# Attention stage of a hybrid decoder trunk: accumulators taken in the order of the text, one query tile less ahead of the key transposes

## The chip, the cores and the metric

The kernel runs on one core of a Trainium2 chip. The metric is the time of one execution on the device in microseconds (us), the median over runs. A core has a matrix engine (TensorE, PE), ScalarE (ACT), VectorE (DVE), GpSimd (POOL) and SyncE (SP). Each works through its own instructions in order, and semaphores order the engines among each other. Matmul results stand in accumulators (PSUM banks), from which ACT or DVE must take them before the bank serves again.

## The reference

One layer of a gated decoder trunk, for a prompt of 1024 tokens and 8 sample sequences of 8 tokens (1088 tokens in all), in float32. A normed, modulated input goes through one wide projection whose columns feed three branches: A (chunked gating), B (attention in a sliding window of 128) and C (mLSTM). Each branch output is gated, projected, and merged. The change lies in the stage that computes branch B, in which parts of A and the gate of B are computed as well:

```python
def sink_attention(qb, kb, vb, mask, sinks):
    logits = jnp.einsum('bnqkgd,bnskd->bnkgqs', qb, kb) * (B_HEAD_DIM ** -0.5)
    logits = jnp.where(mask[None, :, None, None], logits, -jnp.inf)
    mx = jnp.maximum(logits.max(axis=-1), snk)
    p = jnp.exp(logits - mx[..., None])
    den = p.sum(axis=-1) + jnp.exp(snk - mx)
    out = jnp.einsum('bnkgqs,bnskd->bnkgqd', p, vb) / den[..., None]

    q = rmsnorm(q.reshape(bsz, t, B_HEADS, B_HEAD_DIM), qn_g)
    k = rmsnorm(k.reshape(bsz, t, B_KV_HEADS, B_HEAD_DIM), kn_g)
    yb = swa_branch(...) * jax.nn.silu(b_g)
```

There are 8 query heads in 2 groups (one key/value head each), so 16 prompt steps (group, tile of 128 tokens) and 4 sample steps (group, half of the sequences).

## The kernel before, in words

The stages follow each other: start (modulation, norm), the mLSTM branch, its output gates, the attention stage (about 362 to 588 us of the profiled execution), then a long stage of projections and merging up to the output. float32 products are made from pairs of a high and a low half (`hh`/`hlo` for the input, `hl` for a weight slab, read from `raw` in four pieces of 256 KB, cast by ACT and subtracted by DVE).

In the attention stage the key and value tiles come first, with `k_norm` for three tiles at a time and `k_transpose(n)` for one: ACT copies the key tile to `kst`, PE transposes it into an accumulator (two transposes, one per group), ACT casts it to the high half of `KT`, DVE subtracts the low half. From the fourth key tile on, the order of PE is written out by hand (`manual_schedule`): what stands in the text in front is ahead on PE. The other engines' instructions are placed by a scheduler that plans with priorities (`tc.high_priority`) and a model of times.

By hand, a pipeline of steps runs: in round `i` the list `PLAN` calls phase `v` of step i-5, `s` of step i-2, `p` of step i-4, `q` of step i (`y` is only for the samples). Phase `q` transposes a query tile into an accumulator; ACT (high half `hi`) and DVE (low half `lo`) empty it in two rounds (L1074, L1075) into `QT`; in round 7 of a group the sample query tile follows into `QTs`. Phase `s` makes scores in two accumulators, which ACT (`Sm`, L1106) and DVE (copy_predicated, L1107) empty; then come the row maximum, four exps on ACT (L1115), the sum and four normalisations on ACT (L1123). Phase `p` transposes the probabilities and DVE writes them as `Pp` and `Pc`; phase `v` multiplies with the values, and ACT takes the result as `yo` and sends it out.

Between the phases stands `filler`, a sequence of other matmuls of fixed length from which each place takes so many columns (`FILL`): query tiles (`q_tile`, evicted by DVE into `qraw`), tiles of branch A (`av_tile`, into `vn`, with squares on ACT, L1265), and chunks of the gate of B (`bg_chunk`), which ACT evicts twice, as `tb` (tanh, L1236) and `zb` (L1238). POOL sends `zb` out, ACT's queue `yo`. `filler(0, ("q", g, n))` runs the sequence until query tile n of group g is done.

Accumulators: `pg` for filler (three banks), `pk` for key and query transposes and scores (three), `pu` for the transposed probabilities and the output (two). `gt` tiles (`tb`, `zb`, `yo`, `ts`) share five buffers in rotation.

```python
PLAN = ((6, "y", 0), (5, "v", 0), (2, "s", 0.3), (4, "p", 0.3), (0, "q", 0.4))
for n in range(3, 9):
    filler(0, ("q", 0, n - 2))
    k_transpose(n)
```

Of the kernel before, what the change touches and what calls it, by code (L numbers as in the profile page):

```python
# [15 lines left out]
NT = 1088  # L16
# [25 lines left out]
def trunk_kernel(ctx: ExitStack, tc: tile.TileContext, I, O):  # L42
# [37 lines left out]
    def ct(shape, name, dt=F32):  # L80
        return cp.tile(shape, dt, name=name)


# [105 lines left out]
    def gemm_tok_steps(whi, wlo, K, N, n, ah, al, evac):  # L189
        t0, tn = TILES[n]  # L190
        ps = pg()
        for k in range(K):
            if n == 8:
                mm(ps[:, :N], ah[k][:, 1024:1152], whi[:, k], k == 0, False)
                mm(ps[:, :N], ah[k][:, 1024:1152], wlo[:, k], False, k == K - 1)
            else:
                mm(ps[:tn, :N], ah[k][:, t0:t0 + tn], whi[:, k], k == 0, False)
                mm(ps[:tn, :N], ah[k][:, t0:t0 + tn], wlo[:, k], False, False)
                mm(ps[:tn, :N], al[k][:, t0:t0 + tn], whi[:, k], False, k == K - 1)
            if k < K - 1:  # L200
                yield N
        if n == 8:
            t = gt(N, "ts")
            with tc.high_priority():
                S.copy(t[:64], ps[64:128, :N])
                V.tensor_tensor(t[:64], t[:64], ps[:64, :N], ALU.add)
            ps = t
        evac(ps)
        yield N
# [671 lines left out]
    with tc.tile_pool(name="bph", bufs=1, side="right", reuse_waits="tile") as b1:  # L881
# [177 lines left out]
        def q_transpose(g, n):  # L1059
            tn = TILES[n][1]  # L1060
            pq = pk()
            for i in range(2):
                tr(pq[:, tn * i:tn * i + tn], qraw[g][i][:tn, n])
            QT = bt([128, 2, 2, 128], "QT", F32R, bufs=3) if n < 8 else bt([128, 8, 4, 8], "QTs", F32R, bufs=2)
            for r in range(2):
                a, b = slice(64 * r, 64 * r + 64), slice(64 - 64 * r, 128 - 64 * r)
                if n < 8:
                    src = pq[a, 0:256].rearrange("p (i t) -> p i t", i=2)
                    hi, lo = QT[a, :, r], QT[b, :, r]
                else:  # L1070
                    src = pq[a, 0:128].rearrange("p (i b t) -> p b i t", i=2, b=8)
                    hi, lo = QT[a, :, r::2], QT[b, :, r::2]
                with tc.high_priority():
                    S.copy(hi, src)  # L1074
                    newq[0] = V.tensor_tensor(lo, src, hi.bitcast(F32), ALU.subtract).ins  # L1075
            return QT.rearrange("p i r t -> p (i r t)")
# [4 lines left out]
        class Prompt:  # L1081
            def __init__(self, g, n):
                self.g, self.n = g, n
# [11 lines left out]
            def s(self):  # L1095
                g, n, QT, rr = self.g, self.n, self.QT, self.rr
                Sm = bt([128, 4, 128], "Sm", bufs=3)
                for hp_ in range(2):
                    pS = pk()
                    for i in range(2):  # L1100
                        h = 2 * hp_ + i
                        o = pS[:, 256 * i:256 * i + 256]
                        mm(o, QT[:, 128 * h:128 * h + 128], KT[g][0][:, 128 * n:128 * n + 256], True, False)
                        mm(o, QT[:, 128 * h:128 * h + 128], KT[g][1][:, 128 * n:128 * n + 256], False, True)
                    pv = pS.rearrange("p (i w s) -> p i w s", i=2, w=2)
                    S.copy(Sm[:, 2 * hp_:2 * hp_ + 2], pv[:, :, 1])  # L1106
                    V.copy_predicated(Sm[:, 2 * hp_:2 * hp_ + 2], mprv.unsqueeze(1).broadcast_to([128, 2, 128]),  # L1107
                                      pv[:, :, 0] if n > 0 else neg.unsqueeze(1).broadcast_to([128, 2, 128]))
# [17 lines left out]
            def p(self):  # L1126
                n = self.n
                pT = pu_()
                for h in range(4):
                    j = 2 * (h % 2) + h // 2  # L1130
                    tr(pT[:, 128 * j:128 * j + 128], self.Sm[:, h])
                pTv = pT.rearrange("p (h t) -> p h t", h=4)
                if n > 0:
                    self.Pp = bt([128, 4, 128], "Pp")
                    V.scalar_tensor_tensor(self.Pp, mcT.unsqueeze(1).broadcast_to([128, 4, 128]), 0.5, pTv,
                                           ALU.is_lt, ALU.mult)
                self.Pc = bt([128, 4, 128], "Pc")
                V.tensor_tensor(self.Pc, pTv, mcT.unsqueeze(1).broadcast_to([128, 4, 128]), ALU.mult)

            def v(self):  # L1140
# [6 lines left out]
                o = gt(256, "yo")  # L1147
                S.activation(o, pO[:, 0:256], AF.Copy, scale=0.5)
                nc.scalar.dma_start(dy[1, 2 * g:2 * g + 2, :, 128 * n:128 * n + 128].rearrange("f p t -> p f t"),
# [6 lines left out]
        class Sample:  # L1156
# [3 lines left out]
            def q(self):  # L1160
# [12 lines left out]
                self.kT = bt([128, 4, 128], "kTs", tag="QT", bufs=3)  # L1173
                V.tensor_copy(self.kT, pK.rearrange("p (b j) -> p b j", b=4))

            def s(self):
# [6 lines left out]
                Sx = bt([128, 192], "Sx", tag="Sm", bufs=3)  # L1183
                V.tensor_tensor(Sx[:, 0:128], pS[:, 0:128], smask[:, 0:128], ALU.add)
                V.tensor_tensor(Sx[:, 128:192], pS[:, 128:192], smask[:, 160:224] if bg == 0 else smask[:, 128:192], ALU.add)
                nm = bt([128, 1], "nms", bufs=2)
# [10 lines left out]
            def p(self):  # L1197
# [3 lines left out]
                self.PT = bt([128, 256], "PTs", tag="Pc")  # L1201
                V.tensor_copy(self.PT[:, 0:128], pT[:, 0:128])
                V.tensor_copy(self.PT[:64, 128:256], pT[0:64, 128:256])

            def v(self):
# [5 lines left out]
                self.ot = bt([128, 64], "ots", bufs=2)  # L1211
                V.tensor_copy(self.ot, pO[:, 0:64])
                V.tensor_tensor(self.ot, self.ot, pO[:, 64:128], ALU.add)
                V.tensor_scalar(self.ot, self.ot, self.dn, 0.5, ALU.mult, ALU.mult)

            def y(self):
# [3 lines left out]
                for r in range(2):  # L1220
                    S.copy(o[64 * r:64 * r + 64].rearrange("p f (b t) -> p b f t", t=8),
                           py[0:64, 0:128].rearrange("p (b f r t) -> p b f r t", f=2, r=2, t=8)[:, :, :, r])
# [5 lines left out]
        def bg_chunk(f, ci):  # L1228
# [5 lines left out]
            def ev_b(ci, c0, n, ps):  # L1234
                t = gt(n, "tb")
                S.activation(t, ps[:, :n], AF.Tanh, bias=bh[:, CBG + f:CBG + f + 1], scale=0.5)  # L1236
                z = gt(n, "zb")
                S.activation(z, ps[:, :n], AF.Identity, bias=cols[:, CBG + f:CBG + f + 1], scale=1.0)  # L1238
                V.scalar_tensor_tensor(z, t, 1.0, z, ALU.add, ALU.mult)
# [9 lines left out]
        def av_tile(s, n):  # L1249
# [9 lines left out]
            def ev_a(ps):  # L1259
                with tc.high_priority():  # L1260
                    for i in range(2):
                        g = 2 * s + i
                        V.tensor_tensor(vn[g][:tn, n], ps[:tn, 128 * i:128 * i + 128],
                                        avb["b", s][:tn, 128 * i:128 * i + 128], ALU.add)
# [54 lines left out]
        def mix(g):  # L1319
# [3 lines left out]
            for q in range(2):  # L1323
                ps = pk()
                for i in range(4):
                    mm(ps[:, 128 * i:128 * i + 128], vn[g][:, 4 * q + i], WT[:, g], True, True)
                V.scalar_tensor_tensor(sA[g][:, 512 * q:512 * q + 512].rearrange("p (n t) -> p n t", n=4),
                                       ps.rearrange("p (n t) -> p n t", n=4), gcol,
                                       bsb[:, g:g + 1].broadcast_to([128, 4, 128]), ALU.mult, ALU.add)
            ps = pk()  # L1330
            mm(ps[:, 0:64], vn[g][:64, 8], A["WTs"][:, g].rearrange("p b t -> p (b t)"), True, True)
            V.scalar_tensor_tensor(sA[g][:, 1024:NT].rearrange("p (b t) -> p b t", b=8),
                                   ps[:, 0:64].rearrange("p (b t) -> p b t", b=8), gcol,
# [14 lines left out]
        for n in range(9):  # L1348
# [36 lines left out]
        for n in range(3, 9):  # L1385
            filler(0, ("q", 0, n - 2))
            k_transpose(n)
# [19 lines left out]
    keep.close()  # L1407
    one.close()


# [499 lines left out]
```

## Time and profile before

| | |
|---|---|
| median of 3 runs | 1180.49 us (1179.37 to 1182.17) |
| profiled execution | 1182.86 us, its span 1181.1 us |
| mean granted clock of TensorE | 0.999 |
| PE, DVE, ACT busy | 1157.1, 789.1, 489.8 us |
| attention stage, 362 to 588 us: PE, DVE, ACT busy | 222.8, 164.4, 142.8 us |

The span runs from the first to the last instruction; the profiled execution's own time holds some time around it. PE's busy time is that of its matmuls. In a row of the timeline stand the start, the busy time, the engine, the line, the operation with output and inputs, the shapes and how many equal ones follow each other; brackets hold the idle time before it and what ended it. All matmuls have line L88 and all transposes L92, since two helpers record them.

### The profile page before, as it was taken

What the parts mean: (1) busy time and instruction counts of PE and PEld (TensorE: products, weight loads), DVE (VectorE), ACT (ScalarE), POOL (GpSimd) and SP (SyncE); (2) the same over time, 40 slices, a digit from 0 to 9 for tenths busy, and PEclk for the clock granted to TensorE, in tenths of its full rate; (3) what the DMA queues carried; (4) which work ended last, traced back from release to release, by engine and by line L of the source; (5) the groups of instructions that cost most, each with busy time, mean ns of one, the idle gap of its engine ahead of it and who ended that gap; (6) DMA issues with size and microseconds to landing.
All of it is one profiled execution on the core that took longest, in us unless ns stands there. A gap on an engine that the chain in (4) does not pass through costs nothing.

```text
span 1181.1 us, 23183 instructions
## 1 busy us (share of the span) xinstructions
PE 1157.1 (98%) x8942; PEld 1111.5 (94%) x8942; DVE 789.1 (67%) x1865; ACT 489.8 (41%) x1230; POOL 75.7 (6%) x109
## 2 busy tenths in 40 slices
PE   6999999999999999989999999999999999999998
PEld 4799999999999999978998999999999999999998
DVE  5778777655468587876698866555766676668433
ACT  4443455434343368877443433223332343235000
POOL 2000011102024010120100000000000000000000
PEclk9999999999999999999999999999999999999999
DMA  9731222323222211123235125545633354465322
GB/s 300 250 90 37 76 85 64 103 65 103 88 79 75 51 49 40 29 78 90 66 104 149 46 83 154 148 141 149 179 113 114 109 159 119 131 215 182 119 92 72
DMA packets 150773, 129.74 MB, mean 110 GB/s; under 512 B 13613, under 2 KB 140213, under 8 KB 150648
## 3 DMA queue, kind: packets, MB, share of 16 engines
q1 hardware_dynamic: 142984, 118.96, 34.2%
q0 software_dynamic: 2240, 7.08, 1.7%
q10 hardware_dynamic: 5440, 2.23, 0.7%
q8 instruction: 70, 1.15, 0.4%
q14 instruction: 39, 0.32, 0.1%
HBM read 99.39 MB, written 29.82 MB: 109 GB/s over the span
## 4 chain that ended last, share of the span: by engine, by line
PE 86%; DVE 7%; DMA 4%; ACT 2%; issue 1%; SPq 0%; POOL 0%; ACTq 0%; DVEq 0%
PE pg L88 46%; PE pk L88 24%; PE pu L88 13%; PE pk L92 2%; DMA raw<-in_w_in_dram 1%; DMA stage<-dy 1%; PE pu L92 1%; DVE acc L502 1%; DMA xt<-in_x_prompt_dram 1%; DVE hl L128 1%; DMA dy<-stage 0%; DMA fbb<-in_mlstm_f_bias_dram 0%; DVE vv L543 0%; DVE hl L413 0%; DMA mrow<-in_ada_b_dram 0%
## 5 line engine op out<-in xcount | busy, mean ns | idle before, releaser
L88 PE MATMUL pg<-hl,hl 128*128 128x256 f32 (+3 forms) x904 | 277.7, 307 | 0.6 <-DVE hl L413 0.3
L88 PE MATMUL pg<-hh,hl 128*128 128x384 f32 (+1 forms) x912 | 237.4, 335 | 0.4 <-DVE hh L412 0.4
L88 PE MATMUL pg<-hl,hh 128*128 128x256 f32 (+1 forms) x1008 | 177.7, 283 | 0.5 <-DVE zif L547 0.5
L88 PEld LDWEIGHTS pg<-hl,hl 128*128 128x128 f32 x904 | 170.6, 189 | 3.2 <-DVE hl L413 2.4
L88 PEld LDWEIGHTS pg<-hh,hl 128*128 128x128 f32 x912 | 161.8, 189 | 4.1 <-issue 1.9
L88 PEld LDWEIGHTS pg<-hl,hh 128*128 128x128 f32 x1008 | 150.7, 189 | 1.0 <-PE pg L88 0.7
L1441 ACT CAST prod<-raw 128x512 fp32r<-128x512 f32 x76 | 46.8, 620 | 124.7 <-PE pk L88 61.1
L88 PE MATMUL pg<-hh,prod 128*128 128x288 f32 (+1 forms) x400 | 83.9, 289 | 0.2 <-DVE prod L1442 0.2
L88 PE MATMUL pk<-hh,prod 128*128 128x256 f32 (+1 forms) x384 | 78.0, 285 | 0.0
L1442 DVE TENSOR_TENSOR prod<-raw,prod 128x512 fp32r<-128x512 f32 x76 | 51.9, 686 | 27.0 <-ACT prod L1441 26.9
L88 PEld LDWEIGHTS pg<-hh,prod 128*128 128x128 f32 x400 | 65.8, 188 | 1.1 <-DVE comb L1436 0.4
L1605 ACT ACTIVATE tt<-tt,bh 128x288 f32<-128x288 f32 x96 | 49.9, 522 | 37.0 <-DVE tt L1567 14.4
L1441 ACT CAST prod<-comb 128x512 fp32r<-128x512 f32 x60 | 36.9, 616 | 65.3 <-PE pk L88 25.2
L88 PEld LDWEIGHTS pk<-hh,prod 128*128 128x128 f32 x384 | 62.6, 188 | 0.8 <-DVE comb L1436 0.4
L88 PE MATMUL pg<-yh,prod 128*128 128x288 f32 (+1 forms) x288 | 61.3, 290 | 0.5 <-ACT yh L1683 0.5
L88 PE MATMUL pk<-yh,prod 128*128 128x256 f32 (+1 forms) x288 | 58.7, 285 | 0.0
L88 PE MATMUL pg<-hl,prod 128*128 128x288 f32 (+1 forms) x200 | 57.7, 289 | 0.0
L88 PE MATMUL pk<-tc,prod 128*128 128x256 f32 (+1 forms) x408 | 56.3, 287 | 0.0
L88 PE MATMUL pu<-hh,prod 128*128 128x288 f32 (+1 forms) x272 | 56.3, 287 | 0.0
L88 PE MATMUL pg<-tc,prod 128*128 128x288 f32 (+1 forms) x396 | 55.8, 290 | 0.0
L88 PE MATMUL pk<-hl,prod 128*128 128x256 f32 (+1 forms) x192 | 54.6, 284 | 0.0
L88 PEld LDWEIGHTS pk<-tc,prod 128*128 128x128 f32 x408 | 52.7, 188 | 1.3 <-issue 1.3
(553 smaller groups left out, 2649.0 us busy)
## 6 DMA issues: line engine op xcount, KB each, us to landing
raw<-in_w_in_dram SPq DMA_DIRECT2D x124, 256.0 KB
adaraw<-in_ada_w_dram SPq DMA_DIRECT2D x16, 512.0 KB
stage<-dy SPq DMA_DIRECT2D x24, 272.0 KB
dmg<-tt SPq DMA_DIRECT2D x44, 144.0 KB
dmg<-tt SPq DMA_DIRECT2D x44, 128.0 KB
mprev<-dmg SPq DMA_DIRECT2D x32, 144.0 KB
xt<-in_x_prompt_dram SPq DMA_DIRECT2D x8, 512.0 KB
graw<-in_ada_w_dram SPq DMA_DIRECT2D x16, 256.0 KB
```

Of the source, the lines that this page charges most:

```text
L88: T.matmul(out, lhsT=lhsT, rhs=rhs, start=start, stop=stop)
L92: T.transpose(out, in_, ident[:k, :k])
L128: V.tensor_tensor(hl[:, 1, off:off + m], raw[:, :m], hl[:, 0, off:off + m].bitcast(F32), ALU.subtract)
L502: V.scalar_tensor_tensor(acc, xp[:, j:j + XC], cwcol[:, 8 * j + f:8 * j + f + 1], acc, ALU.mult, ALU.add)
L1441: a = S.copy(t[:, 0], x)
L1442: b = V.tensor_tensor(t[:, 1], x, t[:, 0].bitcast(F32), ALU.subtract)
L1605: S.activation(x, x, AF.Tanh, bias=bh[:, b:b + 1], scale=0.5)
```

## The change

A class `Turn` wraps an engine. While it is on, every instruction called through it is issued after the one called through it before, on the same engine (`issue_after` is an ordering for the scheduler; no instruction is added). `SR` wraps ScalarE and `VR` VectorE. In the attention stage every instruction that takes an accumulator of PE goes through them, except the key casts and subtractions and the squares of `vn`; exps, normalisations, reductions and weight casts stay free. It is on from the start of PE's hand-written order to the end of the stage. Second, one query tile less stands in front of the key transposes of tiles 3 to 8.

```diff
+    class Turn:
+        def __init__(self, eng):
+            self.eng, self.last, self.on = eng, None, False
+        def __getattr__(self, name):
+            def call(*a, **k):
+                with (tc.issue_after(self.last) if self.last is not None else nullcontext()):
+                    r = getattr(self.eng, name)(*a, **k)
+                if self.on:
+                    self.last = r.ins
+                return r
+            return call
+    SR, VR = Turn(S), Turn(V)
...
-                        V.tensor_tensor(qraw[g][i][:tn, n], ps[:tn, 128 * i:128 * i + 128],
+                        VR.tensor_tensor(qraw[g][i][:tn, n], ps[:tn, 128 * i:128 * i + 128],
...
-                    S.copy(hi, src)
-                    newq[0] = V.tensor_tensor(lo, src, hi.bitcast(F32), ALU.subtract).ins
+                    SR.copy(hi, src)
+                    newq[0] = VR.tensor_tensor(lo, src, hi.bitcast(F32), ALU.subtract).ins
...
-                    S.copy(Sm[:, 2 * hp_:2 * hp_ + 2], pv[:, :, 1])
-                    V.copy_predicated(Sm[:, 2 * hp_:2 * hp_ + 2], ...
+                    SR.copy(Sm[:, 2 * hp_:2 * hp_ + 2], pv[:, :, 1])
+                    VR.copy_predicated(Sm[:, 2 * hp_:2 * hp_ + 2], ...
...
-                S.activation(t, ps[:, :n], AF.Tanh, bias=bh[:, CBG + f:CBG + f + 1], scale=0.5)
+                SR.activation(t, ps[:, :n], AF.Tanh, bias=bh[:, CBG + f:CBG + f + 1], scale=0.5)
...
         pe.enter_context(tc.manual_schedule(engines={mybir.EngineType.PE}))
+        SR.on = VR.on = True
...
-            filler(0, ("q", 0, n - 2))
+            filler(0, ("q", 0, n - 3))
             k_transpose(n)
...
+    SR.on = VR.on = False
+    SR.last = VR.last = None
```

The same replacement of `S` by `SR` or `V` by `VR` is made for `ts`, `Pp`, `Pc`, `yo`, `kTs`, `Sx`, `PTs`, `ots`, `ys`, `zb`, `vn` and `sA`. In the changed kernel lines move down by 16, and everything called through a `Turn` has line L91.

On ACT, around the transposes of query step 15 (whose tiles are `QT` and, for the samples, `QTs`), before:

```order
L1265 ACTIVATE ts,va<-vn 64x128 x2
L1074 CAST QT<-pk 64x2x128
L1074 CAST QTs<-pk 64x16x8
L1236 ACTIVATE tb<-pg,bh 128x384
L1238 ACTIVATE zb<-pg,cols 128x384
L1115 ACTIVATE Sm,dn<-Sm,nm,r_5769 128x128 x3
L1074 CAST QT<-pk 64x2x128
L1115 ACTIVATE Sm,dn<-Sm,nm,r_5769 128x128
L1148 ACTIVATE yo<-pu 128x256
L1074 CAST QTs<-pk 64x16x8
```

and after:

```order
L91 CAST QT<-pk 64x2x128
L1281 ACTIVATE ts,va<-vn 64x128 x2
L91 CAST QT<-pk 64x2x128
L91 CAST QTs<-pk 64x16x8
L1139 ACTIVATE Sm<-Sm,es 128x128 x4
L1131 ACTIVATE Sm,dn<-Sm,nm,r_5740 128x128 x4
L1135 ACTIVATE es<-es 128x4
L91 CAST QTs<-pk 64x16x8
L91 ACTIVATE tb<-pg,bh 128x384
L91 ACTIVATE zb<-pg,cols 128x384
```

Both `QT` casts now stand ahead of `tb` and `zb`, and the normalisations of an earlier step (`Sm<-Sm,es`) ahead of the next exps (`Sm,dn<-Sm,nm`).

On ACT a step earlier, where a weight slab of the filler is split (`hl<-raw`, four pieces) and the query tile of step 14 is taken, before:

```order
L127 CAST hl<-raw 128x512 x3
L1074 CAST QT<-pk 64x2x128
L847 CAST tc<-tx 128x544
L1123 ACTIVATE Sm<-Sm,es 128x128 x4
L1148 ACTIVATE yo<-pu 128x256
L1106 COPY Sm<-pk 128x256 x2
L1149 DMA dy<-yo 128x2x128
L1074 CAST QT<-pk 64x2x128
L127 CAST hl<-raw 128x512
```

and after:

```order
L91 CAST QT<-pk 64x2x128
L1281 ACTIVATE pg,va<-vn 128x128
L143 CAST hl<-raw 128x512 x3
L1139 ACTIVATE Sm<-Sm,es 128x128 x4
L1281 ACTIVATE pg,va<-vn 128x128
L863 CAST tc<-tx 128x544
L143 CAST hl<-raw 128x512
L1281 ACTIVATE pg,va<-vn 128x128
L91 CAST QT<-pk 64x2x128
```

The fourth piece of the slab, which stood behind the second `QT` cast, now stands ahead of it.

On PE, the third and fourth pair of key transposes (`kst`) among the matmuls of the query tiles, before:

```order
L88 MATMUL pg<-hl,hh_718 128x256 x2
L92 MATMUL pk<-ident,kst 128x128 x2
L88 MATMUL pg<-hl,hl_719 128x256
L88 MATMUL pg<-hl,hh_724 128x256 x2
L88 MATMUL pg<-hl,hl_725 128x256
L88 MATMUL pg<-hl,hh_426 128x256 x2
L88 MATMUL pg<-hl,hl_427 128x256
L92 MATMUL pk<-ident,kst 128x128 x2
L88 MATMUL pg<-hl,hh_432 128x256 x2
```

and after:

```order
L104 MATMUL pg<-hl,hh_426 128x256
L104 MATMUL pg<-hl,hl_427 128x256
L108 MATMUL pk<-ident,kst 128x128 x4
L104 MATMUL pg<-hl,hh_432 128x256 x2
L104 MATMUL pg<-hl,hl_433 128x256
```

The fourth pair has moved up by one query tile and stands directly behind the third. In front of the query transposes of step 15 stand about 22 filler matmuls of 256 columns fewer than before; they come later.

More of the change, by code (lines that the diff above doesn't have):

```diff
@@ L1 @@
-from contextlib import ExitStack
+from contextlib import ExitStack, nullcontext
 import concourse.bass as bass
@@ L204, in gemm_tok_steps @@
             with tc.high_priority():
-                S.copy(t[:64], ps[64:128, :N])
-                V.tensor_tensor(t[:64], t[:64], ps[:64, :N], ALU.add)
+                SR.copy(t[:64], ps[64:128, :N])
+                VR.tensor_tensor(t[:64], t[:64], ps[:64, :N], ALU.add)
             ps = t
@@ L1147, in v @@
                 o = gt(256, "yo")
-                S.activation(o, pO[:, 0:256], AF.Copy, scale=0.5)
+                SR.activation(o, pO[:, 0:256], AF.Copy, scale=0.5)
                 nc.scalar.dma_start(dy[1, 2 * g:2 * g + 2, :, 128 * n:128 * n + 128].rearrange("f p t -> p f t"),
@@ L1173, in q @@
                 self.kT = bt([128, 4, 128], "kTs", tag="QT", bufs=3)
-                V.tensor_copy(self.kT, pK.rearrange("p (b j) -> p b j", b=4))
+                VR.tensor_copy(self.kT, pK.rearrange("p (b j) -> p b j", b=4))
             def s(self):
@@ L1183, in s @@
                 Sx = bt([128, 192], "Sx", tag="Sm", bufs=3)
-                V.tensor_tensor(Sx[:, 0:128], pS[:, 0:128], smask[:, 0:128], ALU.add)
-                V.tensor_tensor(Sx[:, 128:192], pS[:, 128:192], smask[:, 160:224] if bg == 0 else smask[:, 128:192], ALU.add)
+                VR.tensor_tensor(Sx[:, 0:128], pS[:, 0:128], smask[:, 0:128], ALU.add)
+                VR.tensor_tensor(Sx[:, 128:192], pS[:, 128:192], smask[:, 160:224] if bg == 0 else smask[:, 128:192], ALU.add)
                 nm = bt([128, 1], "nms", bufs=2)
@@ L1201, in p @@
                 self.PT = bt([128, 256], "PTs", tag="Pc")
-                V.tensor_copy(self.PT[:, 0:128], pT[:, 0:128])
-                V.tensor_copy(self.PT[:64, 128:256], pT[0:64, 128:256])
+                VR.tensor_copy(self.PT[:, 0:128], pT[:, 0:128])
+                VR.tensor_copy(self.PT[:64, 128:256], pT[0:64, 128:256])
             def v(self):
@@ L1211, in v @@
                 self.ot = bt([128, 64], "ots", bufs=2)
-                V.tensor_copy(self.ot, pO[:, 0:64])
-                V.tensor_tensor(self.ot, self.ot, pO[:, 64:128], ALU.add)
+                VR.tensor_copy(self.ot, pO[:, 0:64])
+                VR.tensor_tensor(self.ot, self.ot, pO[:, 64:128], ALU.add)
                 V.tensor_scalar(self.ot, self.ot, self.dn, 0.5, ALU.mult, ALU.mult)
@@ L1220, in y @@
                 for r in range(2):
-                    S.copy(o[64 * r:64 * r + 64].rearrange("p f (b t) -> p b f t", t=8),
+                    SR.copy(o[64 * r:64 * r + 64].rearrange("p f (b t) -> p b f t", t=8),
                            py[0:64, 0:128].rearrange("p (b f r t) -> p b f r t", f=2, r=2, t=8)[:, :, :, r])
@@ L1262, in ev_a @@
                         g = 2 * s + i
-                        V.tensor_tensor(vn[g][:tn, n], ps[:tn, 128 * i:128 * i + 128],
+                        VR.tensor_tensor(vn[g][:tn, n], ps[:tn, 128 * i:128 * i + 128],
                                         avb["b", s][:tn, 128 * i:128 * i + 128], ALU.add)
```

12 lines of the change are left out of this document (6 added, 6 removed).

## The prediction

> **What bounds the kernel now.** I read the page's busy table first, then the waits of TensorE, then the busy time by stretches, then the timeline where the waits lie. The busy table says which engine everything else must serve.
>
> ```profile
> span 1181.1 us, 23183 instructions
> PE 1157.1 (98%) x8942; PEld 1111.5 (94%) x8942; DVE 789.1 (67%) x1865; ACT 489.8 (41%) x1230; POOL 75.7 (6%) x109
> ```
>
> TensorE (PE) is busy for 1157.1 of 1181.1 us. An edit that removes no matmul can only win back time in which PE stands still or runs at a lower clock. Over the attention stage alone (362 to 588 us) the waits of PE are two rows; the page of the whole span puts them third and fourth, behind start-up.
>
> ```profile
> PE pk L88 <- DVE QT L1075: 1.8, 1, 1.8
> PE pu L92 <- ACT Sm L1123: 1.3, 1, 1.3
> ```
>
> ```profile
> 362.00:588.00 226.00, 222.83 (x1758) 206.43 (x1757) 164.44 (x477) 142.81 (x503) 32.51 (x36) 0.99 0.21 59
> 515.00:522.00 7.00, 3.83 (x24) 3.04 (x22) 3.36 (x14) 6.88 (x28) 2.15 (x2) 1.00 0.21 71
> 522.00:530.00 8.00, 8.00 (x43) 6.99 (x43) 3.90 (x12) 6.15 (x21) 0.55 (x1) 0.79 0.09 24
> 522.80:526.20 3.40, 3.40 (x17) 3.36 (x15) 1.33 (x4) 3.30 (x14) 0.00 (x0) 0.51 0.00 0
> 593.00:645.00 52.00, 51.88 (x430) 47.12 (x428) 47.96 (x95) 22.55 (x49) 0.00 (x0) 1.00 0.40 120
> ```
>
> The columns are the window, its length, busy time of PE, weight loads, DVE (VectorE), ACT (ScalarE) and POOL, the granted clock, the DMA share and GB/s. PE lacks 3.17 us of the 226, all of it between 515 and 522, where ACT is busy for 6.88 of 7.00: the hole is made by ACT. Right behind it the clock is 0.51 for 3.40 us, which costs 3.40 x 0.49 = 1.7 us. So the stage holds about 4.9 us to be won, and no more.
>
> Why ACT was late is in the timeline. Query step 15 puts its transposes into an accumulator; ACT (high half) and DVE (low half) empty it in two rounds; then the bank serves the second half of the scores of step 14.
>
> ```profile
> 511.21 0.65 PE L92 MATMUL pk<-ident,qraw 128*128 128x128 f32 x4
> 511.62 0.37 ACT L1074 CAST QT<-pk 64x256 fp32r<-64x256 f32 x1 [0.64 <-PE pk L92]
> 514.18 0.58 ACT L1236 ACTIVATE tb<-pg,bh 128x384 f32<-128x384 f32 x1 [2.02 <-PE pg L88]
> 514.23 0.42 DVE L1075 TENSOR_TENSOR QT<-pk,QT 64x256 fp32r<-64x256 f32 x1
> 515.08 0.74 PE L88 MATMUL pk<-KT,QT 128*128 128x256 f32 x4
> 515.12 0.49 ACT L1115 ACTIVATE Sm<-Sm,nm,r 128x128 f32<-128x128 f32 x1
> 516.67 0.37 ACT L1074 CAST QT<-pk 64x256 fp32r<-64x256 f32 x1
> 517.07 0.42 DVE L1075 TENSOR_TENSOR QT<-pk,QT 64x256 fp32r<-64x256 f32 x1 [0.98 <-ACT QT L1074]
> 517.64 0.71 PE L88 MATMUL pk<-KT,QT 128*128 128x256 f32 x4 [1.82 <-DVE QT L1075]
> 521.00 2.45 ACT L1123 ACTIVATE Sm<-Sm,es 128x128 f32<-128x128 f32 x8
> 521.46 1.21 PE L92 MATMUL pu<-ident,Sm 128*128 128x128 f32 x4 [1.35 <-ACT Sm L1123]
> ```
>
> The gate eviction `tb` stands ahead of the second `QT` cast. It idles ACT for 2.02 us until a filler chunk ends; exps run next, and the second cast starts only at 516.67. The second wait follows from that: the normalisations of step 12 (L1123) run at 521.00, behind the exps of the next step.
>
> **The change part by part.** No instruction is added to or taken from an engine; order is all that moves.
>
> *Part one, the turn order.* Gate evictions now may not overtake a text-earlier eviction: on ACT, both `QT` casts of step 15 precede `tb`, and the normalisations of step 12 precede the next exps. With the accumulator free, ACT needs 0.37, DVE 0.42, ACT 0.37 and DVE 0.42 us, or 1.6 us for the two rounds. DVE has small reductions between, so I take 2.0. The cover is what PE does from the end of the transposes (511.21 + 0.65 = 511.86) to where it would have begun the second scores (517.64 - 1.82 = 515.82), 4.0 us. So that wait goes, -1.8. The Sm wait goes too, as nothing of the exps is ahead of it any more: -1.35. If a cover fails, the next late thing is again a second score accumulator.
>
> The clock: 0.51 came one stretch after these two waits and nowhere else in the stage (its mean is 0.99), so I let it go with them: -1.7. The Trainium skill, "TensorE: Matmul & The Clock Gate", section "Why this matters for your kernels", warns of PE-idle gaps over about 3 us, one idle window of some 3.4 us bringing half clock. Here the length of the low clock agrees (3.40 us), but the longest single wait, 1.82 us, is under its limit. By the letter of the page the dip is not owed to these waits and would stay, and the sum would be 1.7 us worse.
>
> *What the turn order adds.* A turn makes an eviction wait for an eviction that isn't ready. The nearest such place is the last piece of a weight slab, which the new order puts on ACT (and DVE) ahead of the second `QT` round of step 14. SP may fetch it only after DVE has split the first piece.
>
> ```profile
> 505.23 1.88 DVE L128 TENSOR_TENSOR hl<-raw,hl 128x512 fp32r<-128x512 f32 x3
> 505.93 0.37 SPq L126 DMA_DIRECT2D raw<-in_w_in_dram  x1
> 506.58 1.22 PE L88 MATMUL pk<-KT,QT 128*128 128x256 f32 x8
> 508.26 0.37 ACT L1074 CAST QT<-pk 64x256 fp32r<-64x256 f32 x1
> 508.71 0.62 ACT L127 CAST hl<-raw 128x512 fp32r<-128x512 f32 x1
> ```
>
> Before, that `QT` cast went first, at 508.26; from the fetch's issue to the cast of the piece passed 508.71 - 505.93 = 2.8 us, so the landing takes at most that. If the splits keep their time, piece, cast and DVE round end at 508.71 + 0.62 + 0.37 + 0.42 = 510.1, where PE wants the bank for step 15 at about 509.8 (its 511.21, less 2.6 us for some 22 query matmuls that no longer stand ahead of it, at 0.12 us each, plus the 1.2 us of part two). That is 0.3 us; if the splits come earlier, nothing. For step 14's scores I allow another 0.3 for a DVE that is behind with `Pp` and `Pc`. Sum +0.6; bounds 0 and 3.2 (both old waits back in new places).
>
> The other queues: SP's slab fetch follows the DVE split as before; the DMAs of `yo` (ACT's queue) and of `zb` (POOL) follow their evictions, whose buffers are five in rotation. A transfer of `zb` lands 2.2 us after issue:
>
> ```profile
> dsg<-zb POOLq DMA_DIRECT2D x1, 192.0 KB, 2.2
> ```
>
> A gate chunk of 384 columns is 24 matmuls and takes over 4 us of PE (0.17 us each: two take 0.51, one 0.34), so a buffer is back before its next turn; cost 0.
>
> ```profile
> 510.51 0.51 PE L88 MATMUL pg<-hh,hl 128*128 128x384 f32 x2
> 510.86 0.34 PE L88 MATMUL pg<-hl,hl 128*128 128x384 f32 x1
> ```
>
> *Part two, key transposes one query tile earlier.* Six `k_transpose` calls move (tiles 3 to 8), each with one kst copy and two casts on ACT, two subtractions on DVE, two transposes on PE, no DMA. PE does the same work. But the fourth pair now stands right behind the third, and there are three accumulators: it needs the first pair's bank.
>
> ```profile
> 374.32 0.38 PE L92 MATMUL pk<-ident,kst 128*128 128x128 f32 x2
> 374.37 1.28 DVE L128 TENSOR_TENSOR hl<-raw,hl 128x512 fp32r<-128x512 f32 x2
> 375.01 0.28 PE L88 MATMUL pg<-hl,hl 128*128 128x256 f32 x1
> 375.12 0.40 PE L88 MATMUL pg<-hl,hh 128*128 128x256 f32 x2
> 375.93 0.29 DVE L1021 TENSOR_TENSOR KT<-pk,KT 128x128 fp32r<-128x128 f32 x1
> 377.83 0.38 PE L92 MATMUL pk<-ident,kst 128*128 128x128 f32 x2
> 380.58 0.56 DVE L1005 TENSOR_TENSOR kn<-kn,kqg 128x384 f32<-128x384 f32 x1
> 380.88 0.38 PE L92 MATMUL pk<-ident,kst 128*128 128x128 f32 x2
> 383.93 0.38 PE L92 MATMUL pk<-ident,kst 128*128 128x128 f32 x2
> ```
>
> DVE empties that bank at 375.93 + 0.29 = 376.22, behind the same two slab splits as before, since DVE's order there is unchanged. PE, which reached the fourth pair at 377.83, now has it behind the second pair (374.32), two matmuls and the third pair, so reaches it about 375.0: +1.2 us. Bounds: 0 if DVE comes to that row earlier, 2.9 (1.2 and a clock dip of 1.7). A query tile is 24 matmuls at 0.12 us (375.01 to 375.12 is one), 2.8 us; from the pair at 377.83 to that at 380.88 there is one tile. Tiles 4 and 5 follow after a whole tile of such work. The tile that is not done ahead is done among the steps: the filler is one sequence of fixed length, so PE has the same work and 0 is added. Tile 6 takes tile 5's slot at 383.93, 2.8 us behind the last factor on the keys (380.58 + 0.56 = 381.14), which covers a copy and costs 0.
>
> **Sum.** -1.8 - 1.35 - 1.7 + 0.6 + 1.2 = -3.0 us. The profiled execution took 1182.86 us, 2.4 us above the median of the runs shown (1180.49) and above all three. I take the median less 3.0: 1177.5. Behind the stage PE is full (51.88 of 52.00 us from 593 to 645), so an earlier end of attention is passed on to the end of the kernel, as far as DVE (47.96 of 52.00) keeps up.
>
> **The rivals.** A measurement of this kernel tells about 0.2% (2.4 us) from no change, so "faster" begins at 1178.1 and "slower" at 1182.9.
>
> 1. *All of it is won*: the fourth key pair is covered, the slab piece is early, and about 4.9 us go: 1175.6. For it: ACT and DVE have slack in the stage (142.81 and 164.44 of 226). Against it: the bank of the first keys is bound by an unmoved DVE row.
> 2. *The hole moves*: the two waits come back in other places, because ACT was busy for 6.88 of 7.00 us from 515 to 522 and its work is only permuted; or DVE, busy for 47.96 of 52.00 us from 593 to 645, eats the lead. Then -3.0 shrinks to nothing: 1180.5.
> 3. *The clock's 1.7 us is not won.* The low clock followed the waits, but one dip is little to judge by: it may have another cause and stay; the three runs, lower than the profiled one, may not have had it; or the wait at 375, with six transposes just before and behind it, makes a new one (0.51 began right behind four transposes, the row at 521.46). Each leaves -3.0 + 1.7 = -1.3: 1179.2. The first would follow from the Trainium skill's section on idle gaps above. Its section "Part 4: PE-mode transpose" says that the clock gate doesn't count transposes as busy in the same way, which would speak for the last; no run here has settled either.
> 4. *Slower by the slab piece*: the turn order holds ACT in front of a landing 256 KB piece with evictions queued behind it, at both slab changes of the interleaved steps. Where the piece is issued 2 us later than I assume, PE waits for 2.0 us more and the clock dips (1.7): 3.7 us at each place, -3.0 + 7.4 = +4.4: 1184.9. It decides (1182.9) from a delay of 1.0 us with a dip at both places (2 x 2.7 - 3.0 = +2.4). For it: ACT waits in order, 2.02 us for `tb` here. Against it: the piece had landed by 508.71 and PE has other matmuls queued for most of that time.
>
> **How the numbers follow.** Forecast with its own range 1176.5 to 1178.7: 0.34, most of it (0.30) below 1178.1. Rival 1: 0.17. Rival 2: 0.12. Rival 3: 0.20. Rival 4: 0.17. Faster 0.30 + 0.17 = 0.47; same 0.04 + 0.12 + 0.20 = 0.36; slower 0.17. The range takes in all but rival 4: from 1174.8 (rival 1 less 0.8 for the runs' own scatter, 1179.4 to 1182.2) to 1182.8.
>
> **What the profile of the changed kernel would show.** Among the waits of PE the QT row (1.8) and the Sm row (1.3) are gone; in their place stands one of about 1.2 us on KT near 375, and one below 0.6 on QT between 505 and 515. The stretch behind 515 has the clock at 1.00. On ACT, the two `QT` casts of step 15 lie under 1.5 us apart, ahead of `tb`. I am wrong if PE shows a new wait of over 1.5 us in the stage, if a low clock stands anywhere in it, or if PE's busy share from 593 to 645 falls below 51.5 us.

## The result and the profile after

The changed kernel takes 1182.67 us (median of 20 runs, 1180.01 to 1184.6), the kernel before 1180.45 us (median of 20, 1179.08 to 1184.45): ratio 1.0017, 95% interval 1.0011 to 1.0024. It is 2.2 us slower where 3.0 us faster was forecast.

The page of the changed kernel alone would mislead:

```profile
span 1178.3 us, 23181 instructions
PE 1154.0 (98%) x8942; PEld 1108.6 (94%) x8942; DVE 788.4 (67%) x1865; ACT 489.4 (42%) x1230; POOL 75.1 (6%) x109
```

Its span is 2.8 us shorter than that of before, against the medians. The profiled execution of the changed kernel, 1180.01 us, is the fastest of its 20; that of before, 1182.86 us, lies 2.4 us above its median. What differs by chance lies outside the stage that was changed. So the stage is measured by itself, from its first key transposes to the first matmul of the next stage, changed kernel (lines L108, L104) and before (L92, L88) each:

```profile
369.17 0.38 PE L108 MATMUL pk<-ident,kst 128*128 128x128 f32 x2
586.56 0.40 PE L104 MATMUL pg<-hh,prod 128*128 128x288 f32 x1
```

```profile
371.03 0.38 PE L92 MATMUL pk<-ident,kst 128*128 128x128 f32 x2
587.84 0.40 PE L88 MATMUL pg<-hh,prod 128*128 128x288 f32 x1
```

That is 586.56 - 369.17 = 217.4 us after and 587.84 - 371.03 = 216.8 before; a second profiled execution of each gave 217.3 and 215.3. The stage is 0.5 to 2.1 us longer. The waits of PE in it (362 to 588 us) after the change:

```profile
PE pk L108 <- DVE KT L1037: 1.2, 1, 1.2
PE pk L108 <- DVE QT L91: 1.1, 1, 1.1
PE pk L108 <- DVE Sm L91: 0.8, 1, 0.8
PE pg L104 <- ACT pg L1281: 0.7, 1, 0.7
PE pu L104 <- DVE Pp L91: 0.5, 1, 0.5
PE pk L108 <- ACT pg L1281: 0.4, 1, 0.4
```

The two waits of before (1.8 and 1.3) are gone, and six others add up to 4.7 us. (A seventh row, 0.2 us on `prod`, lies behind the stage; the kernel before has it too.) The first is that of the fourth key pair. The next two lie around query step 15. How they come about is in the timeline of PE, ACT and DVE between 502 and 513 us; the query tile of step 14 is transposed at 502.47, and PE wants its bank again at 510.28 (511.36 less the wait of 1.08):

```profile
502.47 0.38 PE L108 MATMUL pk<-ident,qraw 128*128 128x128 f32 x2
502.89 0.37 ACT L91 CAST QT<-pk 64x256 fp32r<-64x256 f32 x1 [1.23 <-PE pk L108]
504.07 1.66 ACT L143 CAST hl<-raw 128x512 fp32r<-128x512 f32 x3 [0.51 <-PE pg L104]
504.41 0.28 DVE L91 TENSOR_TENSOR vn<-pg,avb 128x128 f32<-128x128 f32 x1
505.64 1.28 ACT L1139 ACTIVATE Sm<-Sm,es 128x128 f32<-128x128 f32 x4
506.82 0.26 ACT L1281 ACTIVATE pg<-vn 128x128 f32<-128x128 f32 x1
508.12 0.27 DVE L91 TENSOR_TENSOR vn<-pg,avb 128x128 f32<-128x128 f32 x1
508.42 0.42 DVE L91 TENSOR_TENSOR QT<-pk,QT 64x256 fp32r<-64x256 f32 x1
509.34 0.62 ACT L143 CAST hl<-raw 128x512 fp32r<-128x512 f32 x1 [1.60 <-DMA raw<-in_w_in_dram]
510.29 0.37 ACT L91 CAST QT<-pk 64x256 fp32r<-64x256 f32 x1
510.79 0.43 DVE L91 TENSOR_TENSOR QT<-pk,QT 64x256 fp32r<-64x256 f32 x1
511.36 0.41 PE L108 MATMUL pk<-ident,qraw 128*128 128x128 f32 x2 [1.08 <-DVE QT L91]
512.59 0.34 PE L108 MATMUL pk<-ident,qraw 64*128 64x64 f32 x2 [0.81 <-DVE Sm L91]
```

The high half of `QT` is ready at 503.26. Its low half runs only at 508.42, because in the text a branch A tile (`vn`) is evicted ahead of it, and that eviction has two additions on DVE with a square on ACT between them, into the same bank. The second addition comes after the square; the square stands on ACT behind three slab casts and four normalisations and runs at 506.82. By the turn DVE may not let `QT` pass meanwhile. DVE doesn't stand idle here: it takes slab splits and other work that has no turn, and comes to the second addition at 508.12, 1.04 us after the square's end. At other places of the steps (396 to 530 us) it does stand and wait for squares:

```profile
DVE vn L91 <- ACT pg L1281: 2.4, 3, 1.4
```

Then the slab's fourth piece is waited for (1.60 us), and PE pays 1.08 and 0.81 us.

### The profile page after: what moved, and what is told of

The parts are those of the page before. It is cut to its first block, busy times and chain, and to the rows that moved or that the text cites. A ratio compares the mean times of both kernels' runs of the same rounds, so it can differ in the third digit from the quotient of the medians.

```text
span 1178.3 us, 23181 instructions
## 1 busy us (share of the span) xinstructions
PE 1154.0 (98%) x8942; PEld 1108.6 (94%) x8942; DVE 788.4 (67%) x1865; ACT 489.4 (42%) x1230; POOL 75.1 (6%) x109
## 4 chain that ended last, share of the span: by engine, by line
PE 82%; DVE 9%; DMA 4%; ACT 3%; issue 1%; SPq 0%; ACTq 0%; POOL 0%; DVEq 0%
PE pg L104 43%; PE pk L104 24%; PE pu L104 13%; PE pk L108 2%; DMA raw<-in_w_in_dram 1%; DVE hl L144 1%; DMA stage<-dy 1%; ACT Sm L1131 1%; DVE acc L518 1%; PE pu L108 1%; DMA xt<-in_x_prompt_dram 1%; DMA dy<-stage 0%; DVE vv L559 0%; DVE xT L406 0%; DVE hl L429 0%
## 5 line engine op out<-in xcount | busy, mean ns | idle before, releaser
L104 PE MATMUL pg<-hl,hl 128*128 128x256 f32 (+3 forms) x904 | 277.0, 307 | 0.6 <-DVE hl L429 0.2
L104 PE MATMUL pg<-hh,hl 128*128 128x384 f32 (+1 forms) x912 | 236.1, 333 | 0.4 <-DVE hh L428 0.4
L104 PE MATMUL pg<-hl,hh 128*128 128x256 f32 (+1 forms) x1008 | 177.5, 283 | 0.7 <-ACT pg L1281 0.7
L104 PEld LDWEIGHTS pg<-hl,hl 128*128 128x128 f32 x904 | 170.2, 188 | 3.2 <-DVE hl L429 2.4
L104 PEld LDWEIGHTS pg<-hh,hl 128*128 128x128 f32 x912 | 160.9, 188 | 4.1 <-issue 2.3
L104 PEld LDWEIGHTS pg<-hl,hh 128*128 128x128 f32 x1008 | 150.5, 189 | 1.2 <-ACT pg L1281 0.9
L104 PE MATMUL pg<-hh,prod 128*128 128x288 f32 (+1 forms) x400 | 83.9, 289 | 0.2 <-DVE prod L1461 0.2
L104 PE MATMUL pk<-hh,prod 128*128 128x256 f32 (+1 forms) x384 | 78.0, 285 | 0.0
L104 PEld LDWEIGHTS pg<-hh,prod 128*128 128x128 f32 x400 | 65.8, 188 | 1.1 <-issue 0.4
L104 PEld LDWEIGHTS pk<-hh,prod 128*128 128x128 f32 x384 | 62.6, 188 | 0.8 <-issue 0.4
L104 PE MATMUL pg<-yh,prod 128*128 128x288 f32 (+1 forms) x288 | 61.0, 290 | 0.0
L104 PE MATMUL pk<-yh,prod 128*128 128x256 f32 (+1 forms) x288 | 58.7, 285 | 0.0
L104 PE MATMUL pg<-hl,prod 128*128 128x288 f32 (+1 forms) x200 | 57.7, 289 | 0.0
L104 PE MATMUL pk<-tc,prod 128*128 128x256 f32 (+1 forms) x408 | 56.3, 287 | 0.0
L104 PE MATMUL pu<-hh,prod 128*128 128x288 f32 (+1 forms) x272 | 56.3, 287 | 0.0
L104 PE MATMUL pg<-tc,prod 128*128 128x288 f32 (+1 forms) x396 | 55.8, 290 | 0.0
L104 PE MATMUL pk<-hl,prod 128*128 128x256 f32 (+1 forms) x192 | 54.6, 284 | 0.0
L104 PEld LDWEIGHTS pk<-tc,prod 128*128 128x128 f32 x408 | 52.7, 188 | 1.3 <-issue 1.3
```

Of the source, the lines that this page charges most:

```text
L104: T.matmul(out, lhsT=lhsT, rhs=rhs, start=start, stop=stop)
```

## The experiments

Each ratio is to the kernel before on the same chip; the waits are those of PE in the stage, from a profile of each kernel.

**The kernel before again.**

> The kernel before, unchanged, to see how its runs scatter and with what granted clock each goes. Theory A (the low clock of 1.7 us in the profile of before was the exception: that execution took 1182.86 us, the median is 1180.45): most runs have clock 1.000 and about 1180 us, and the profile has the two waits of 1.8 and 1.3 us, mostly without a low clock behind them. Rival B (the low clock comes in every run, and the profiled execution was long for another reason): most runs have clock 0.999 or less.

Ratio 0.9998 (0.9985 to 1.0011). Its profile has the QT wait, no Sm wait, and half clock right behind the wait:

```profile
PE pk L88 <- DVE QT L1075: 1.8, 1, 1.8
```

```profile
518.20:521.60 3.40, 3.33 (x13) 3.36 (x14) 1.05 (x5) 3.33 (x15) 0.00 (x0) 0.50 0.29 96
```

Theory A falls, and the count is as Rival B said: 10 of the 35 runs of before in this comparison have a clock of 1.000, the others less, and (1 - clock) x span averages 2.8 us over them. That mean doesn't tell where in the program the clock was low; the start has its share (last section). The 1.3 us wait on Sm isn't there in every execution.

**One part at a time.** The turn alone has `n - 2` again; the keys alone is the kernel before with `n - 3`.

```diff
-            filler(0, ("q", 0, n - 3))
+            filler(0, ("q", 0, n - 2))
```

> The changed kernel with the old filler in front of the key transposes (n - 2): the turn order alone. Theory A (1.2 us come from the fourth key pair's bank, and the wait for step 15's bank comes from a slab piece whose time is fixed by its fetch): the 1.2 us wait at the keys goes, query steps come about 1.4 us later against the slab piece, so its wait of 1.1 us shrinks to near nothing; about 1180 us. Rival B (the turn order delays evictions everywhere): the keys' wait goes, the others stay or move; about 1181.5 us.

> The kernel before with one query tile less in front of the key transposes, without the turn order. Theory A: the 1.2 us wait for KT appears at 375, the waits of 1.8 and 1.3 us around 515 stay in some form (their place among the filler shifts by a tile): about 1181.7 us, +1.2. Rival B (the two parts need each other): the shifted filler makes the old waits longer or adds new ones, over 1183 us.

Turn alone: 0.9990 (0.9978 to 1.0003), 1180.09 us. Keys alone: 0.9979 (0.9969 to 0.9989), 1178.35 us where before takes 1180.86. Its waits:

```profile
PE pk L92 <- DVE KT L1021: 1.2, 1, 1.2
PE pk L92 <- DVE Sm L1107: 0.7, 1, 0.7
PE pk L88 <- DVE QT L1075: 0.7, 1, 0.7
```

Neither theory said that. The part that I had priced at +1.2 us gains 2.5 by itself: it does bring the KT wait, but it also moves all steps one query tile forward among the fillers, and there the waits around 515 to 521 and the low clock don't arise. The turn alone came out at the time that its Theory A named, with the KT wait gone and 0.2 us left of the QT wait at step 15; its gain of 0.8 us is unclear. Together they lose 2.2: the parts don't add.

**The slab's fourth piece behind the query tile.** In `load_pieces` the fourth piece's cast and subtraction are kept back and issued after the two `QT` rounds.

```diff
+            if q == 3 and SR.on and newq[0] is not None:
+                pend.append((hl, raw, off, m))
...
                 self.QT = q_transpose(g, n)
+                split_pending()
```

> The changed kernel, but the split of a slab's fourth piece (the ACT cast and the DVE subtraction) is ordered behind both rounds of the next query tile. Theory A (evictions stood behind a piece whose fetch had not landed): the waits at 511 and 512.6 (1.08 and 0.81 us) and that at 437 (0.48) go or fall under 0.3 each, the KT wait of 1.2 stays; about 2 us less than the changed kernel, 1180.5 us. Rival B (the engines are simply late with the evictions, whatever stands ahead): the waits move, and the time stays at 1182.7 us.

1182.28 us, ratio 1.0011 (1.0001 to 1.0022); against the changed kernel's 1.0017 that is no clear gain. QT and Pp are no longer waited for, but a wait of 1.5 us on normalisations, at 537 us, took their place, as Rival B said:

```profile
PE pu L108 <- ACT Sm L1153: 1.5, 1, 1.5
PE pk L108 <- DVE KT L1052: 1.2, 1, 1.2
PE pk L108 <- DVE Sm L91: 0.8, 1, 0.8
PE pg L104 <- ACT pg L1296: 0.4, 1, 0.4
```

So the piece, my prediction's candidate, is in the row of causes but isn't the one that sets the time.

**The turn on one engine.** The changed kernel with `SR.on = True` alone, and with `VR.on = True` alone.

> The changed kernel with the turn order on ScalarE alone (VectorE's evictions are free again); one query tile less in front as in the change. Without any turn this is 1178.4, with both 1182.7 us. Theory A (ScalarE's turn costs: evictions stand behind others that aren't ready): about 1182 us, with the waits of about 1 us near 480 and 511. Rival B (VectorE's turn costs): about 1178.5 us, with the waits of the kernel with keys alone (KT 1.2, QT 0.7, Sm 0.7).

> The changed kernel with the turn order on VectorE alone. Theory A (ScalarE's turn costs): about 1178.5 us. Rival B (VectorE's turn costs: copy_predicated, Pp and Pc stand behind a filler tile's evictions in the order of the text): about 1182 us, waits on Sm and Pp by DVE. Rival C (it takes both, since each waits for the other's half): both of these kernels stay near 1179 to 1180 us.

ScalarE's turn: 0.9992 (0.9980 to 1.0003), 1180.33 us. VectorE's: 1.0030 (1.0016 to 1.0043), 1184.58 us, with these as its longest waits:

```profile
PE pk L108 <- DVE QT L91: 1.7, 1, 1.7
PE pk L108 <- DVE KT L1037: 1.2, 1, 1.2
PE pk L108 <- DVE Sm L91: 0.9, 1, 0.9
PE pu L108 <- ACT Sm L1139: 0.7, 1, 0.7
PE pu L104 <- DVE Pp L91: 0.7, 1, 0.7
```

Rival B holds in the main: VectorE's turn costs most, and more without ScalarE's than with it. ScalarE's turn came out 2 us above the 1178.5 that Rival B named, so it may cost something too; its interval overlaps that of the keys alone. Part of what VectorE's turn loses is the clock, low right behind its QT and Sm waits (3.40 x 0.47 = 1.6 us):

```profile
515.70:519.10 3.40, 3.40 (x14) 2.77 (x14) 3.21 (x11) 2.82 (x8) 1.37 (x2) 0.53 0.00 0
```

**The KT wait taken away.** The query tile is left out before the ninth pair, whose bank has long been free.

```diff
-            filler(0, ("q", 0, n - 3))
+            filler(0, ("q", 0, min(n - 2, 5)))
```

> The changed kernel, with the query tile that is left out in front of the key transposes taken from before the ninth pair instead of the fourth: the steps still start one tile earlier, but no pair stands directly behind one whose bank is needed. Theory A (the KT wait of 1.2 us adds): that wait is gone, the others stay, 1181.4 us. Rival B (work behind that wait was late anyway): the other waits grow by as much, 1182.5 us.

> The kernel before with the query tile left out in front of the ninth pair, no turn order. Theory A: as the kernel with keys alone (1178.4 us) less the KT wait of 1.2: 1177.2 us, the fastest so far. Rival B: the 1.2 us come back as longer waits at steps (QT near 449, Sm near 511), 1178.4 us.

In the changed kernel: 1.0002 (0.9989 to 1.0016), the KT wait gone and the five others within 0.2 us of what they were. Without the turn: 0.9975 (0.9963 to 0.9987), against 0.9979 with the wait; 1.2 us lie within these intervals, so the wait's price isn't seen in the times. It is seen in the profiled stage: 215.4 us instead of 217.4 in the changed kernel, 213.1 instead of 214.2 without the turn.

**What VectorE waits for in its turn.** First, both additions of a branch A tile before both squares; then the same with the late fourth piece; then the additions out of the turn (`V` for `VR`); last, squares behind without any turn.

```diff
                         VR.tensor_tensor(vn[g][:tn, n], ps[:tn, 128 * i:128 * i + 128],
                                         avb["b", s][:tn, 128 * i:128 * i + 128], ALU.add)
+                    for i in range(2):
+                        g = 2 * s + i
                         S.activation(ps[:tn, 128 * i:128 * i + 128], vn[g][:tn, n], AF.Square,
```

> The changed kernel, but a branch A tile is evicted by both additions of VectorE first and then squared twice by ScalarE, where it was addition, square, addition, square. Theory D (in the turn, the first QT subtraction of step 14 stands behind the second addition of a branch A tile, which waits for ScalarE's square of the first; the square stands on ScalarE behind three slab casts, so QT's high half of 502.9 gets its low half only at 508.4): the QT wait of 1.08 us at 511, the waits of 0.74 and 0.39 near 480 and 444 go or fall under 0.3, the KT wait stays: 1180.3 us, 2.4 less than the changed kernel. Rival B (VectorE is late by its own load in this order, whatever it waits for): the wait at 511 stays at 0.8 or more, 1182.2 us.

> As the kernel with the squares last, and in addition the slab's fourth piece is split behind both QT rounds. Theory D (the second addition was the cause, the piece only stood in the row behind it): no further gain, 1180.3 us. Theory A, what is left of it (the piece costs on its own): 0.5 to 1 us less than with the squares last.

> The changed kernel, with the additions of branch A (vn) left out of VectorE's turn; they still wait for the squares. Theory D: nothing of QT or Sm stands behind them by rule any more, so the waits fall as with the squares last: about 1180.3 us. Rival (the turn of Sm, Pp, Pc is what costs): 1182 us or more.

> Without any turn: the kernel with the query tile left out in front of the ninth key pair (1178.4), with the squares of branch A last. Theory D says that the second addition blocks VectorE here too, only less (it is free to be passed by the scheduler's order): 0 to 0.7 us gain, 1178.0 us, the wait on Sm near 510 (0.8) smaller. Rival: QT near 448 waits behind exps of ScalarE and that near 510 behind Pp, so nothing changes: 1178.4 us.

Squares last: 0.9991 (0.9978 to 1.0004). With the piece late too: 0.9996 (0.9982 to 1.0010), no more. Additions free: 0.9990 (0.9976 to 1.0004). No turn, squares last: 0.9985 (0.9971 to 0.9999), no gain over 0.9975. With the squares last the additions stand together and the low half of `QT` follows its transposes (at 505.15) by 2.2 us instead of 6.0; the QT wait at step 15 is gone, the wait on Sm behind it has grown from 0.8 to 1.5:

```profile
505.15 0.38 PE L108 MATMUL pk<-ident,qraw 128*128 128x128 f32 x2
506.16 0.48 DVE L91 TENSOR_TENSOR vn<-pg,avb 128x128 f32<-128x128 f32 x2
507.37 0.42 DVE L91 TENSOR_TENSOR QT<-pk,QT 64x256 fp32r<-64x256 f32 x1
514.68 0.31 PE L108 MATMUL pk<-ident,qraw 64*128 64x64 f32 x2 [1.50 <-DVE Sm L91]
```

**The same on one chip.** The changed kernel again; with the additions free and the gap at the ninth pair; and the turn without the additions and without the second edit.

> The changed kernel itself, beside the next two on one chip. Its ratio to the kernel before was 1.0017; the kernels with vn out of the turn and with the squares last stood at 0.999 on another chip. Theory D (vn in VectorE's turn costs 2 to 3 us): the changed kernel again at 1.001 to 1.002, 2 to 3 us above the same kernel with vn free. Rival (the chips differ): it comes out within 1 us of them.

> The changed kernel with vn left out of VectorE's turn and with the query tile taken from before the ninth key pair: both faults that were found are mended. If the KT wait's 1.2 us add to vn's 2.7: ratio 0.998, the time of the kernel with the keys' gap alone (1178.4 where the kernel before takes 1181.1). If the turn order itself is worth the 1.8 and 1.3 us of waits that it was made out to remove: below that, 0.996. If the waits only move: 0.999.

> The turn order alone, without vn in it, with the filler in front of the key transposes as before: what the turn order gives without its fault and without the other edit. With vn it was 0.999. Theory D: vn costs here too, 0.998 or less. Rival (vn only blocks where the steps come a tile earlier, as a slab's split then falls between): 0.999 as with vn.

The changed kernel: 1183.32 us, 1.0022 (1.0011 to 1.0033). With both mended: 1178.84 us, 0.9982 (0.9967 to 0.9997), 4.5 us less on the same chip, of which the KT wait is 1.2. Its waits are QT 0.8 and Pp 0.7. The comparison that changes the additions alone, 1.0002 with the gap at the ninth pair and 0.9982 without the additions in the turn, gives 2.4 us, between two chips. The third kernel was a surprise: 1.0012 (0.9997 to 1.0027). The second wait of before is back, in ACT, PE and the clock, beside smaller waits on QT and Sm:

```profile
517.51 0.48 ACT L1131 ACTIVATE Sm<-Sm,nm,r 128x128 f32<-128x128 f32 x1
521.38 1.29 ACT L1139 ACTIVATE Sm<-Sm,es 128x128 f32<-128x128 f32 x4
521.87 1.19 PE L108 MATMUL pu<-ident,Sm 128*128 128x128 f32 x4 [1.57 <-ACT Sm L1139]
```

```profile
523.10:526.50 3.40, 3.40 (x15) 3.36 (x14) 2.08 (x4) 1.37 (x5) 0.00 (x0) 0.50 0.16 58
```

The normalisations (`Sm<-Sm,es`) aren't evictions, so they have no turn. Where they stand is the planner's choice, and here they stand behind the next step's exps once more.

**That order alone.** A step's exps are issued after the normalisations of the step before.

```diff
+                        if newN[0] is not None:
+                            od.enter_context(tc.issue_after(newN[0]))
                         newS[0] = S.activation(Sm[:, h], Sm[:, h], AF.Exp, ...
...
+                    newN[0] = S.activation(Sm[:, h], Sm[:, h], AF.Copy, scale=es[:, h:h + 1]).ins
```

> The turn order without vn and without the second edit (1.0012 of the kernel before), and a prompt step's exps are issued after the normalisations of the step before it. Theory E (the wait on Sm was never the turn's to remove: the normalisations are outside it, ran at 521.4 behind the next step's exps, and the low clock followed that wait): the Sm wait of 1.57 us near 520 goes, no low clock in the stage, ratio 0.998 to 0.999. Rival (ACT is simply full there; ordered normalisations push the evictions back): a wait of 1 to 2 us on QT or the scores instead, ratio 1.001.

> The kernel before with that one order (exps after the previous step's normalisations) and no turn. Theory E: the wait on Sm (1.3) goes or stays gone; the QT wait of 1.8 us, made by the gate eviction ahead of the second QT cast, stays: at most 1 us gained, ratio 0.999. Rival: the QT wait grows by what the normalisations now take ahead of it (1.3 us), ratio 1.001.

> The fastest kernel so far (query tile left out before the ninth key pair, no turn, ratio 0.9975) with that order as well. Its waits are Sm by VectorE 0.8 and QT 0.7; the QT wait near 448 stood behind two steps' exps. Theory E: QT's second cast then comes between them or no later, ratio 0.997 to 0.9975. Rival: normalisations that wait for VectorE's reciprocal hold up ACT, ratio 0.999.

On the turn without the additions: 0.9990 (0.9978 to 1.0002) from 1.0012 on another chip, the 1.57 us wait and the low clock gone. On the kernel before, without any turn: 1179.21 us, 0.9978 (0.9966 to 0.9989), 2.5 us less where Theory E allowed at most 1, with a single wait left:

```profile
PE pk L88 <- DVE QT L1075: 1.8, 1, 1.8
```

The second execution of before had this wait alone too, and a stage of 215.3 us, here 214.0; the half clock behind the wait is there and not here. So what the order itself gained isn't separated from the clock.

With the query tile left out before the ninth pair: 1176.83 us where before takes 1181.72, 0.9955 (0.9938 to 0.9972), the fastest time of all, from six runs, and better than Theory E said. Its stage takes 212.1 us where the same kernel without this order takes 213.1; the rest of its lead over 0.9975 isn't seen there. The waits left (`prod` behind the stage):

```profile
PE pk L88 <- DVE QT L1075: 0.8, 1, 0.8
PE pg L88 <- DVE prod L1446: 0.2, 1, 0.2
```

**The stage by itself.** Measured as in the section on the result, in one profiled execution where no second is given, the stage takes (half clock is in both of before and where the table says so):

| kernel | stage, us |
|---|---|
| before | 216.8 and 215.3 |
| changed | 217.4 and 217.3 |
| keys alone | 214.2 |
| turn alone | 214.3 |
| changed, ScalarE's turn only | 214.9 |
| changed, VectorE's turn only | 220.5, with half clock |
| changed, fourth piece late | 216.5 |
| changed, squares last | 215.0 |
| changed, additions free | 214.8 |
| changed, gap at the ninth pair | 215.4 |
| changed, additions free and gap at the ninth pair | 213.6 |
| turn alone, additions free | 218.1, with half clock |

On top of the second edit the turn adds 3.2 us; with the additions free 0.5 is left, with the squares last 0.8. With the old filler the same additions stand in the turn and the stage is short (214.3), so the loss needs both edits.

## Why the prediction was wrong, point by point

- *The two old waits go (-1.8, -1.35).* They did in the changed kernel. But the turn isn't the only way: with the second edit alone neither stands around 515 to 521 either. That the Sm wait goes "as nothing of the exps is ahead of it any more" was read from one order of the planner; the turn doesn't hold it, and with the additions free and the old filler it came back with 1.57 us. This step was right by its number and wrong by its reason.
- *What the turn order adds (+0.6, bounds 0 and 3.2).* This step failed. It measured 3.5 us: 1.08, 0.81, 0.74, 0.48 and 0.39. (Against the second edit alone, which has waits of 0.74 on QT and 0.75 on Sm, the turn adds 2.0 us of waits, and 3.2 us to the stage.) I priced one place, the slab's piece, and took the low half of `QT` to be prompt. The cause that the runs bear out is VectorE's turn (1.0030 alone, against 0.9992 for ScalarE's): `QT` may not pass a `vn` addition that must follow a square, which has no turn and stands behind slab casts on ACT. Taking the additions out of the turn, or making them independent of the square, brings the kernel back to 0.999. The slab's piece has a share: ACT waits 1.60 us for it, and with the piece late the QT wait goes as well. But the time stayed, as a wait of 1.53 us came elsewhere, so that share isn't separated.
- *The key transposes (+1.2).* The wait is there with 1.21 us, and it goes with the gap at the ninth pair:

```profile
374.07 0.29 DVE L1037 TENSOR_TENSOR KT<-pk,KT 128x128 fp32r<-128x128 f32 x1
374.51 0.41 PE L108 MATMUL pk<-ident,kst 128*128 128x128 f32 x2 [1.21 <-DVE KT L1037]
```

- *"PE has the same work and 0 is added" for the tile done later.* Same work, but not 0: the second edit alone gained 2.5 us, as all steps meet other fillers. Missing this term, I took the part that gains for the part that costs.
- *The clock (-1.7).* No low clock stands in the stage in either profile of the changed kernel; in before it stands there in both (0.99 over the stage). In the changed kernel:

```profile
362.00:588.00 226.00, 221.04 (x1750) 204.07 (x1751) 163.30 (x475) 142.84 (x505) 30.75 (x34) 1.00 0.21 59
```

In the timed runs no gain from it can be told: (1 - clock) x span averages 1.9 and 3.2 us in two sets of the changed kernel and 2.2 to 3.1 us in five of before.
- *The sum.* By profile: -3.17 of old waits, +4.7 of new ones, -1.7 of clock, or -0.2; the stage grew by 0.6. The remaining 0.8 isn't in the rows of waits; most of it is in PE's busy time, which fell by 1.0 us in the stage (213.6 to 212.6) where the clock alone stood for 1.7. Against the second execution of before, without the Sm wait, the stage grew by 2.1, and the medians say 2.2. My base was an execution with one wait more than the second of the same kernel.
- *Behind the stage PE stays full.* Right, and DVE kept up:

```profile
593.00:645.00 52.00, 52.00 (x429) 46.88 (x428) 48.69 (x98) 23.00 (x51) 0.00 (x0) 1.00 0.38 115
```

- *The rivals.* The slower one named evictions behind an unready predecessor, which is the right family, but on ACT and by the fetch of a piece; the larger part was on DVE and by a square. Rival 2, the hole that moves, is nearest to what happened, but it saw the waits come back in full and no more.
- *The signs.* None of the three that were to show the forecast wrong appeared: the longest new wait is 1.21 us, the clock is 1.00, PE is full from 593 to 645. They watched for one long wait, and several short ones made the loss. The row on QT between 505 and 515, named as below 0.6, measured 1.08.

What stays open: why the turn with the additions free loses to the turn with them when the second edit is absent (1.0012 against 0.9990, intervals that overlap). The profiles differ by where the planner put the normalisations; that these follow from the additions was not traced.

## What to carry to other kernels

An in-order rule over one kind of instruction makes every unready member a gate for all that follow, and it says nothing about the instructions left out of it: before turning evictions into a queue, list for each what it waits for, on the other engine too. One precise order, put where the chain of waits names two instructions in the wrong sequence (here exps ahead of the normalisations of the step before), did no worse than a general one (0.9978 against 0.9990, intervals that overlap). And moving filler in front of a pipeline shifts every later meeting of the two, so it is priced by a profile of that part alone, not by its matmuls.

## What the hardware showed beyond that

Half clock came for 3.40 us after single waits far under 3 us: behind 1.83 us in the second execution of before, behind 1.57 in the turn with the additions free, behind 1.54 with the squares last and the piece late (0.52 from 536.20 to 539.60). It did not come behind 1.83 us in the kernel before with ordered normalisations, nor behind 1.53 us with the late piece. In the first execution of before it came behind 1.35 us and not behind the 1.82 us ahead of that. So the limit that the Trainium skill gives on a single idle gap ("TensorE: Matmul & The Clock Gate", section "Why this matters for your kernels") was not what decided here, and what did is not settled.

Between the two profiled executions of the changed kernel most of the scatter lies ahead of the stage: where the clock was low for 6.8 us in the start (which costs 3.4), the first key transposes came at 373.91, in the execution shown above at 369.17, while the stage differs by 0.1 us. In the kernel before it is the other way round: 371.03 and 371.65, and 1.5 us in the stage.

```profile
24.10:30.90 6.80, 6.80 (x39) 3.39 (x43) 1.53 (x4) 1.27 (x3) 0.00 (x0) 0.50 1.11 339
373.91 0.38 PE L108 MATMUL pk<-ident,kst 128*128 128x128 f32 x2
```
